# Hybrid decoder layer: RWKV head pairs with alpha and r side by side, r H of both heads in one product, the state's update in two halves of 64 columns

## The chip, the cores and the metric

The kernel runs on 1 core of one Trainium2 chip. The metric is the device time of one execution in microseconds (us). A core has five engines with a queue each: TensorE (PE; its weight loads are shown as PEld), VectorE (DVE), ScalarE (ACT), GpSimd (POOL) and SyncE (SP), which here issues all DMAs. Each works its instructions off in order, and waits on semaphores for the others. DVE, ACT and PE can reach PSUM, where matmuls put their results.

## The reference, cut to what matters

One layer: RMSNorm, one input projection whose columns go to a convolution group, a sparse attention group and an RWKV-7 group; an output projection; a gated MLP. 1024 tokens, all float32. The change lies in the RWKV group (4 heads of 64):

```python
def step(S, inp):
    r_t, w_t, k_t, v_t, kk_t, a_t = inp
    sa = jnp.einsum('bhvk,bhk->bhv', S, -kk_t)
    S = S * w_t[:, :, None, :] + sa[..., None] * (kk_t * a_t)[:, :, None, :] + v_t[..., None] * k_t[:, :, None, :]
    return S, jnp.einsum('bhvk,bhk->bhv', S, r_t)
```

The kernel does not scan 1024 tokens. It cuts them into 16 chunks of 64 and writes the recurrence within a chunk as matrices: with the decays multiplied in, alpha = -kk (shifted decay), r = r (decay), and "keys" k and kk*a divided by the decay, a chunk needs the masked products of keys with alpha (GA) and of keys with r (GR), the inverse of a triangular matrix taken from GA, and the state H at its start.

## The kernel before, in words

**Units.** The RWKV work is cut into four units (j, h): j is a pair of heads (128 channels), h a half of the tokens (8 chunks). Each unit has three steps, named in one string that orders the first phase: `lora r0 S00 conv taps V00 S01 keys q C00 V01 r1a cmp0 r1b cmp1 r1c S10 C01 V10 S11 C10 V11 C11`. S is `rwkv_prep` and `rwkv_mats`, V `rwkv_solve`, C `rwkv_chain`; the other names are projections (with L229's matmuls) and the convolution's 31 taps.

**S.** `rwkv_prep` loads k, r and v, makes the decays (L415 to L428), the norm of the keys (L437 to L446), alpha (L457, L458, into the right half of the tile VAc beside v), r times decay (L461) and the keys BK (L468, L469). `rwkv_mats` multiplies keys by alpha (L493, 16 products of 64 columns for 8 chunks and 2 heads), masks them into GA (L497), sends the lower corners to DRAM and back (L503, L506), and does the same for r into GR. It transposes VAc and BK into VA and KB (L517, L518). Then GpSimd inverts 32x32 triangles by 31 steps of two instructions, L528 and L530; DVE copies the result transposed (L532), and it goes to DRAM.

**V.** `rwkv_solve` loads the inverses back (L543 to L547) and does five groups of small matmuls (L550, L556, L563, L571, L575), with an ACT copy after each.

**C.** `rwkv_chain` goes through the 8 chunks: AT times H (L591), DVE adds into VA (L592), KB times VA (L596) is the state's update, which DVE adds to the decayed state (L601, L603); the output is GR times VA (L609) plus r times H (L611) for each head. H is 128x128 with a head in each diagonal block and zeros beside them. Group norm and gate follow (L617 to L638).

**What sets the order.** The kernel is written in a tile framework. While it is built, a scheduler gives each engine its queue by a timeline of its own: of the instructions that are ready there, the one with the highest priority goes next, and S, V and C carry a high priority. A tile is put into a free slot of its pool; RWKV tiles of 128x512 share 20 slots (`rb`). So an edit in `rwkv_prep` moves work of all groups in all queues. After the first phase come eight attention tiles, then the output projection, then the MLP (Strassen-like products of 7 instead of 8) up to the end.

**The convolution's taps.** Of its two channel halves DVE does one (L270, L272: 31 instructions of 128x1024); of the other, ACT scales each tap (L278) and POOL adds it (L274, L279: 60 adds of 128x512). A projection needs its weights split into a high and a low part: ACT writes `whi` (L120), DVE `wlo` (L121), both with 2 buffers.

Of the kernel before, what the change touches and what calls it, by code (L numbers as in the profile page):

```python
# [16 lines left out]
P = 128  # L17


class K:  # L20
# [370 lines left out]
    def rwkv_prep(self, j, h):  # L391
# [61 lines left out]

        for q in range(2):
            sl = slice(q * 256, q * 256 + 256)
            al = VAc[q][:, :, 1, :]
            v.scalar_tensor_tensor(al[:, :, 1:64], c3(kk[:, sl])[:, :, 1:64], -1.0, c3(Pt[:, sl])[:, :, 0:63], op0=ALU.mult, op1=ALU.mult)  # L457
            v.tensor_scalar(al[:, :, 0], c3(kk[:, sl])[:, :, 0], -1.0, None, op0=ALU.mult)  # L458
        u.r = self.rb([P, 8, 64], name="rP")
        u.AT = self._t(self.mc, [P, 8, 64], F32, "at", "AT")  # L460
        et(u.r, c3(rr), c3(Pt), op=ALU.mult)  # L461

# [18 lines left out]
    def rwkv_mats(self, u):  # L481
# [5 lines left out]
        u.GA, u.GR = [], []  # L487
        for x, G in enumerate((u.GA, u.GR)):
            pts = [self.bank(u.tp) for _ in range(2)]
            for c in range(8):  # L490
                for hp in range(2):
                    r = slice(hp * 64, hp * 64 + 64)
                    pe.matmul(pts[hp][:, c * 64:c * 64 + 64], u.BK[c // 4][r, c % 4].rearrange("p a t -> p (a t)"),  # L493
                              u.r[r, c, :] if x else u.VAc[c // 4][r, c % 4, 1, :], start=True, stop=True)
            for hp in range(2):
                Gm = self.rb([P, 8, 64], name="GR" if x else "GA")
                v.tensor_tensor(Gm, pts[hp].rearrange("p (a b) -> p a b", b=64),  # L497
                                self.gmask[:, x * 64:x * 64 + 64].unsqueeze(1).to_broadcast([P, 8, 64]), op=ALU.mult)
                G.append(Gm)
                if not x:  # L500
                    for blk in range(2):
                        p0 = blk * 16 + hp * 8
                        nc.sync.dma_start(dn[p0:p0 + 8].rearrange("p s t -> s p t"), Gm[64 + blk * 32:96 + blk * 32, :, blk * 32:blk * 32 + 32])  # L503
# [75 lines left out]
    def rwkv_chain(self, u):  # L579
# [7 lines left out]
        for c in range(8):  # L587
# [6 lines left out]
            if not last:  # L594
                pt = self.bank("rw")
                pe.matmul(pt[:, 0:P], KB, VA, start=True, stop=True)  # L596
# [8 lines left out]
            yo = (c // 2) * P  # L605
            for hp in range(2):
                x = slice(hp * 64, hp * 64 + 64)
                o = py[ro, yo + hp * 64:yo + hp * 64 + 64]
                pe.matmul(o, u.GR[hp][:, c, :], VA[:, x], start=True, stop=H is None)  # L609
                if H is not None:  # L610
                    pe.matmul(o, u.r[:, c, :], H[:, x], start=False, stop=True)  # L611
# [790 lines left out]
```

## Time and profile before

| | us |
|---|---|
| runs (3) | 1509.61, 1513.1, 1527.16; median 1513.1 |
| profiled execution, its own time | 1503.66 |
| its span | 1501.9 |
| PE / DVE / ACT / POOL busy | 1418.3 / 1006.5 / 682.5 / 498.9 |

The page of the profile has the busy time of each engine and a strip of 40 slices, each 37.5 us, with tenths of busy time. The first phase reaches to about 377 us, the attention tiles to 743, the output projection to about 860, and the MLP to the end. In a row of the timeline the two numbers are the start and the length in us of a run of equal instructions (x16 is 16 of them); the bracket is the idle time of the engine before it, with what ended it. A float32 matmul of the program shows as two matmul records. Line numbers are those of the kernel before.

### The profile page before, as it was taken

The page shows a single profiled execution, that of the slowest core. Times are in us where ns is not written, and L with a number is a line of the kernel's source. Part 1 is how long each engine was busy: PE and PEld are TensorE (multiplying, and loading weights), DVE is VectorE, ACT ScalarE, POOL GpSimd, SP SyncE. Part 2 cuts the span into 40 slices and gives each one's busy share as a digit, 9 for nine tenths or more (in the row PEclk, how much of TensorE's full clock was granted, in tenths as well). Part 3 has the DMA queues.
Part 4 walks back from the last instruction along what each step waited for, and adds up shares of the span by engine and source line. Part 5 has one row for each costly group of instructions (what it writes and reads, how often), then busy time and mean ns, then how long its engine had stood idle before and what let it go on. Part 6 is the DMA issues. An engine that isn't in the chain of part 4 may idle for free.

```text
span 1501.9 us, 22963 instructions
## 1 busy us (share of the span) xinstructions
PE 1418.3 (94%) x8025; PEld 1125.8 (75%) x8025; DVE 1006.5 (67%) x2171; ACT 682.5 (45%) x1361; POOL 498.9 (33%) x607
## 2 busy tenths in 40 slices
PE   6999688999899999999799899999999999999997
PEld 5887466777677777667588677788888888888886
DVE  6347696454577777689436876775775876666675
ACT  5431255534266555668523443333333344445463
POOL 1003787910432273240100133444443452113310
PEclk9999887999699999999999999999999999999999
DMA  6132223434812442553642122332332333986623
GB/s 186 36 113 74 46 77 96 148 88 120 227 26 72 143 136 74 163 171 104 182 155 78 52 80 80 106 113 91 106 112 84 106 113 125 390 284 212 203 92 112
DMA packets 206680, 186.71 MB, mean 124 GB/s; under 512 B 56355, under 2 KB 145764, under 8 KB 206564
## 3 DMA queue, kind: packets, MB, share of 16 engines
q1 hardware_dynamic: 206564, 185.24, 39.6%
q8 instruction: 63, 1.03, 0.3%
q14 instruction: 53, 0.43, 0.1%
HBM read 126.99 MB, written 58.20 MB: 123 GB/s over the span
## 4 chain that ended last, share of the span: by engine, by line
PE 80%; DVE 10%; DMA 3%; POOL 2%; issue 2%; ACT 1%; SPq 1%; DVEq 0%; POOLq 0%; ACTq 0%
PE mm L229 13%; PE gb L229 12%; PE rw L229 11%; PE ga L229 9%; PE gc L229 8%; PE tr L229 5%; PE tr L918 4%; PE av L926 4%; PE mm L893 2%; PE mm L894 2%; POOL sT L530 1%; DVE pp L897 1%; POOL sx L528 1%; DMA x<-in_x_dram 1%; DVE cacc L272 1%
## 5 line engine op out<-in xcount | busy, mean ns | idle before, releaser
L229 PE MATMUL mm<-hT,whi 128*128 128x512 f32 x608 | 200.5, 410 | 0.0
L229 PE MATMUL mm<-hT,wlo 128*128 128x512 f32 x304 | 125.3, 414 | 20.2 <-DVE wlo L121 20.2
L229 PEld LDWEIGHTS mm<-hT,whi 128*128 128x128 f32 x608 | 117.4, 195 | 28.3 <-issue 1.4
L921 ACT ACTIVATE pT<-tr 128x512 f32<-128x512 f32 (+1 forms) x152 | 79.2, 534 | 54.4 <-PE tr L918 52.7
L926 PE MATMUL av<-pT,V 128*64 128x128 f32 x1056 | 95.3, 289 | 2.3 <-ACT pT L921 2.3
L279 POOL TENSOR_TENSOR cacc<-cacc,ctap 128x512 f32<-128x512 f32 x60 | 91.8, 1552 | 14.8 <-ACT ctap L278 14.6
L1072 POOL TENSOR_TENSOR S<-wraw,wr 128x512 f32<-128x512 f32 x22 | 28.5, 1296 | 194.7 <-DVE or L107 93.5
L918 PE MATMUL tr<-idn,pp 128*128 128x128 f32 x528 | 91.2, 291 | 1.9 <-DVE pp L911 1.7
L121 DVE TENSOR_TENSOR sp<-rb,sp 128x512 fp32r<-128x512 f32 x66 | 57.3, 868 | 48.6 <-ACT sp L120 48.3
L229 PEld LDWEIGHTS mm<-hT,wlo 128*128 128x128 f32 x304 | 59.4, 196 | 38.2 <-DVE wlo L121 21.3
L229 PE MATMUL rw<-sp,sp 128*128 128x512 f32 x330 | 86.2, 389 | 0.0
L229 PE MATMUL tr<-sp,sp 128*128 128x512 f32 x330 | 85.9, 389 | 0.0
L229 PE MATMUL rw<-woh,mix 128*128 128x512 f32 x240 | 79.1, 406 | 5.3 <-DVE xn L994 5.3
L893 PE MATMUL mm<-KH,QS 128*128 128x512 f32 (+2 forms) x192 | 76.8, 406 | 5.8 <-DVE mx L897 3.6
L918 PEld LDWEIGHTS tr<-idn,pp 128*128 128x128 f32 x528 | 57.0, 143 | 31.6 <-issue 28.0
L926 PEld LDWEIGHTS av<-pT,V 128*64 128x64 f32 x1056 | 59.1, 138 | 28.8 <-issue 13.7
L120 ACT ACTIVATE sp<-rb 128x512 fp32r<-128x512 f32 x66 | 41.6, 630 | 74.4 <-PE tr L229 36.5
L121 DVE TENSOR_TENSOR sp<-b,sp 128x512 fp32r<-128x512 f32 x88 | 69.7, 802 | 6.0 <-ACT sp L120 5.9
L229 PEld LDWEIGHTS rw<-sp,sp 128*128 128x128 f32 x330 | 61.9, 188 | 13.2 <-ACT sp L120 0.4
L229 PEld LDWEIGHTS tr<-sp,sp 128*128 128x128 f32 x330 | 61.9, 188 | 12.9
L911 DVE TENSOR_SCALAR pp<-pp,sm 128x640 f32<-128x640 f32 (+7 forms) x128 | 68.3, 573 | 1.0
L904 ACT ACTIVATE pp<-pp,nm 128x640 f32<-128x640 f32 (+3 forms) x64 | 57.6, 902 | 23.8 <-DVE nm L902 22.5
(457 smaller groups left out, 3699.5 us busy)
## 6 DMA issues: line engine op xcount, KB each, us to landing
wr<-in_ffn_w_gate_dram SPq DMA_DIRECT2D x44, 256.0 KB
wraw<-in_ffn_w_up_dram SPq DMA_DIRECT2D x44, 256.0 KB
pdS<-prod SPq DMA_DIRECT2D x44, 256.0 KB
b<-pdS SPq DMA_DIRECT2D x44, 256.0 KB
rb<-tdT SPq DMA_DIRECT2D x44, 256.0 KB
pdA<-prod SPq DMA_DIRECT2D x33, 256.0 KB
b<-pdA SPq DMA_DIRECT2D x33, 256.0 KB
wraw<-in_w_in_dram SPq DMA_DIRECT2D x30, 256.0 KB
```

The source lines that it names most:

```text
L120: self.nc.scalar.activation(hi, src, AF.Copy)
L121: getattr(self.nc, eng).tensor_tensor(lo, src, hi.bitcast(F32), op=ALU.subtract)
L229: mm = lambda l, r, **k: self.nc.tensor.matmul(out, l, r, skip_group_check=more, **k)
L279: nc.gpsimd.tensor_tensor(t[:, o:o + 512], t[:, o:o + 512], z, op=ALU.add)
L893: pe.matmul(pts[g][:, 0:n], QS[:, r, g, :], KH[g][hf][:, ks], start=True, stop=False)
L894: pe.matmul(pts[g][:, 0:n], QS[:, r, g, :], KL[g][hf][:, ks], start=False, stop=True)
L904: s.activation(Ps[g], Ps[g], AF.Exp, bias=nm[:, g:g + 1], scale=-1.0, accum_out=sm[:, g:g + 1])
L911: v.tensor_scalar(Ps[g], Ps[g], sm[:, g:g + 1], None, op0=ALU.mult)
L918: pe.transpose(pt[:, o:o + P], Ps[g][:, kt * P:kt * P + P], self.idn)
L921: s.activation(pT[:, 0:n], pt[:, 0:n], AF.Copy)
L926: pe.matmul(av[g * 64:g * 64 + 64, r * P:r * P + P], self.V[kk // 2][:, kk % 2, vo + g * 64:vo + g * 64 + 64], pT[:, o:o + P], start=first ...
L1072: gp.tensor_tensor(t, x, y, op=op)
```

## The change

1. alpha is written by DVE into a new tile AR ([128, 4 chunks, 2, 64], two per unit); ACT copies it into VAc, and copies r into AR's other half. 2. `rwkv_mats` multiplies keys by alpha and r at once: per half unit q (4 chunks) and head one product of 128 columns, 16 per unit in place of 32 of 64 columns. The masks are 8 DVE instructions of 256 columns per unit in place of 4 of 512. 3. The state's update KB x VA is two products, with 64 columns of KB each. 4. r x H is one product of 128 columns for both heads, ahead of GR x VA, in place of two of 64.

```diff
--- before.py
+++ after.py
@@ -451,14 +451,18 @@
         et(k2, k2, rk, op=ALU.mult)
         e.tensor_scalar(tha, tha, 0.5, 0.5, op0=ALU.mult, op1=ALU.add)
 
+        u.AR = [self.rb([P, 4, 2, 64], name="AR") for _ in range(2)]
         for q in range(2):
             sl = slice(q * 256, q * 256 + 256)
-            al = VAc[q][:, :, 1, :]
+            al = u.AR[q][:, :, 0, :]
             v.scalar_tensor_tensor(al[:, :, 1:64], c3(kk[:, sl])[:, :, 1:64], -1.0, c3(Pt[:, sl])[:, :, 0:63], op0=ALU.mult, op1=ALU.mult)
             v.tensor_scalar(al[:, :, 0], c3(kk[:, sl])[:, :, 0], -1.0, None, op0=ALU.mult)
+            s.activation(VAc[q][:, :, 1, :], al, AF.Copy)
         u.r = self.rb([P, 8, 64], name="rP")
         u.AT = self._t(self.mc, [P, 8, 64], F32, "at", "AT")
         et(u.r, c3(rr), c3(Pt), op=ALU.mult)
+        for q in range(2):
+            s.activation(u.AR[q][:, :, 1, :], u.r[:, q * 4:q * 4 + 4, :], AF.Copy)
 
         et(kk, kk, tha, op=ALU.mult)
         u.BK = []
@@ -484,23 +488,23 @@
         dn = self.dram.tile([32, 32, 32], F32, name=f"dn{u.j}{u.h}")
         u.dt = self.dram.tile([16, 32, 4, 8], F32, name=f"dt{u.j}{u.h}")
         u.dtt = self.dram.tile([32, 8, 4, 32], F32, name=f"dtt{u.j}{u.h}")
-        u.GA, u.GR = [], []
-        for x, G in enumerate((u.GA, u.GR)):
+
+        u.GA, u.GR = ([self.rb([P, 8, 64], name=n) for _ in range(2)] for n in ("GA", "GR"))
+        for q in range(2):
             pts = [self.bank(u.tp) for _ in range(2)]
-            for c in range(8):
+            for c in range(4):
                 for hp in range(2):
                     r = slice(hp * 64, hp * 64 + 64)
-                    pe.matmul(pts[hp][:, c * 64:c * 64 + 64], u.BK[c // 4][r, c % 4].rearrange("p a t -> p (a t)"),
-                              u.r[r, c, :] if x else u.VAc[c // 4][r, c % 4, 1, :], start=True, stop=True)
-            for hp in range(2):
-                Gm = self.rb([P, 8, 64], name="GR" if x else "GA")
-                v.tensor_tensor(Gm, pts[hp].rearrange("p (a b) -> p a b", b=64),
-                                self.gmask[:, x * 64:x * 64 + 64].unsqueeze(1).to_broadcast([P, 8, 64]), op=ALU.mult)
-                G.append(Gm)
-                if not x:
-                    for blk in range(2):
-                        p0 = blk * 16 + hp * 8
-                        nc.sync.dma_start(dn[p0:p0 + 8].rearrange("p s t -> s p t"), Gm[64 + blk * 32:96 + blk * 32, :, blk * 32:blk * 32 + 32])
+                    pe.matmul(pts[hp][:, c * P:c * P + P], u.BK[q][r, c].rearrange("p a t -> p (a t)"),
+                              u.AR[q][r, c].rearrange("p a t -> p (a t)"), start=True, stop=True)
+            for x, G in enumerate((u.GA, u.GR)):
+                for hp in range(2):
+                    v.tensor_tensor(G[hp][:, q * 4:q * 4 + 4, :], pts[hp].rearrange("p (a b) -> p a b", b=P)[:, :, x * 64:x * 64 + 64],
+                                    self.gmask[:, x * 64:x * 64 + 64].unsqueeze(1).to_broadcast([P, 4, 64]), op=ALU.mult)
+        for hp in range(2):
+            for blk in range(2):
+                p0 = blk * 16 + hp * 8
+                nc.sync.dma_start(dn[p0:p0 + 8].rearrange("p s t -> s p t"), u.GA[hp][64 + blk * 32:96 + blk * 32, :, blk * 32:blk * 32 + 32])
         N = self.sN.rearrange("p (a b) -> p a b", b=32)
         for g in range(4):
             nc.sync.dma_start(N[g * 32:g * 32 + 32], dn)
@@ -593,7 +597,8 @@
             last = u.h == 1 and c == 7
             if not last:
                 pt = self.bank("rw")
-                pe.matmul(pt[:, 0:P], KB, VA, start=True, stop=True)
+                for x in (slice(0, 64), slice(64, 128)):
+                    pe.matmul(pt[x, 0:P], KB[:, x], VA, start=True, stop=True)
                 Hn = self.rH[c % 2]
                 for hp in range(2):
                     x = slice(hp * 64, hp * 64 + 64)
@@ -603,12 +608,11 @@
                         v.scalar_tensor_tensor(Hn[x, x], H[x, x], u.PC[x, c:c + 1], pt[x, x], op0=ALU.mult, op1=ALU.add)
             ro = slice((c % 2) * 64, (c % 2) * 64 + 64)
             yo = (c // 2) * P
+            if H is not None:
+                pe.matmul(py[ro, yo:yo + P], u.r[:, c, :], H, start=True, stop=False)
             for hp in range(2):
                 x = slice(hp * 64, hp * 64 + 64)
-                o = py[ro, yo + hp * 64:yo + hp * 64 + 64]
-                pe.matmul(o, u.GR[hp][:, c, :], VA[:, x], start=True, stop=H is None)
-                if H is not None:
-                    pe.matmul(o, u.r[:, c, :], H[:, x], start=False, stop=True)
+                pe.matmul(py[ro, yo + hp * 64:yo + hp * 64 + 64], u.GR[hp][:, c, :], VA[:, x], start=H is None, stop=H is None or hp == 1)
             H = None if last else Hn
         self.H = H
```

The scheduler's queues move with it. Three places follow, in the rows that the built programs have; a number after a name is that of a buffer, and lines after L460 stand 4 lower after the change in most places (L532 became L536, L528 L532, L530 L534).

POOL, the end of the first unit's inverse (S00); before:

```order
L528 TENSOR_TENSOR sx<-sN,sT 128x49
L530 TENSOR_TENSOR sT<-sT,sx 128x7x7
L528 TENSOR_TENSOR sx<-sN,sT 128x42
L530 TENSOR_TENSOR sT<-sT,sx 128x6x7
L528 TENSOR_TENSOR sx<-sN,sT 128x35
```

and after the change:

```order
L532 TENSOR_TENSOR sx<-sN,sT 128x49
L274 TENSOR_SCALAR cacc_1582<-cy_1515,par 128x1024
L534 TENSOR_TENSOR sT<-sT,sx 128x7x7
L279 TENSOR_TENSOR cacc_1582<-cacc_1582,ctap_1615 128x512
L279 TENSOR_TENSOR cacc_1582<-cacc_1582,ctap_1618 128x512
L532 TENSOR_TENSOR sx<-sN,sT 128x42
L279 TENSOR_TENSOR cacc_1582<-cacc_1582,ctap_1621 128x512
L534 TENSOR_TENSOR sT<-sT,sx 128x6x7
L279 TENSOR_TENSOR cacc_1582<-cacc_1582,ctap_1624 128x512
L532 TENSOR_TENSOR sx<-sN,sT 128x35
```

Before, all 62 instructions of the inverse stand in a row, and the first tap (L274) follows them. Now L274 and 13 taps of L279 stand among the last 13 of the 62.

DVE, the transposed copy of that inverse (tile sTT) and the splits of weights (wlo) about it; before:

```order
L257 SCALAR_TENSOR_TENSOR cy_1521<-ev_1455,mm_279_1535 128x512
L272 SCALAR_TENSOR_TENSOR cacc_1587<-cy_1389,par,cacc_1587 128x1024
L532 COPY sTT<-sT 128x256
L121 TENSOR_TENSOR wlo_2255<-wraw_2252,whi_2254 128x512
L272 SCALAR_TENSOR_TENSOR cacc_1587<-cy_1389,par,cacc_1587 128x1024
```

and after the change:

```order
L121 TENSOR_TENSOR wlo_2393<-wraw_2389,whi_2392 128x512
L272 SCALAR_TENSOR_TENSOR cacc_1581<-cy_1383,par,cacc_1581 128x1024
L443 COPY cum_2026<-rrn_2043 128x512
L536 COPY sTT<-sT 128x256
L121 TENSOR_TENSOR wlo_2400<-wraw_2396,whi_2399 128x512
```

The copy stood behind 14 of DVE's 30 taps of L272, and stands behind 28 now; five wlo splits, the norm of unit S01 (L439 to L443) and three evictions of keys (L686) were moved ahead of it. On PE, 14 projection matmuls stood between unit S01's L437 and the first product of V00 (L550), and 127 do now.

PE, the decays and the key norm of unit S10 (products L415, L419, L437, L446); before, two pieces of the queue:

```order
L575 MATMUL rw_2942<-W_2931,sN 64x64 x8
L415 MATMUL rw_3413<-lora_771,lw_w 128x512
L229 MATMUL mm_591_3245<-hT_120,wlo_3242 128x512
...
L437 MATMUL rw_3432<-bones,cum_3422 128x2 x4
L768 MATMUL tr_566_3138<-hx_3036,w2k 64x64
L229 MATMUL mm_606_3341<-hT_120,whi_3337 128x512
```

and after the change:

```order
L579 MATMUL rw_2931<-W_2920,sN 64x64 x8
L415 MATMUL rw_3402<-lora_771,lw_w 128x512
L419 MATMUL rw_3406<-lora_771,lw_w 128x512
L437 MATMUL rw_3421<-bones,cum_3411 128x2 x4
L446 MATMUL rw_3444<-idn,cum_3411 128x128 x4
L843 MATMUL mm_4522<-kcmp_4433,q_816_4515 128x128 x4
L897 MATMUL mm_4542<-KH_4487,QS_4517 128x256
```

Between these four products of S10 stood 72 projection matmuls, and nothing stands there now; the projections are all ahead of L415, and the first attention products follow L446.

## Rows read from the trace of the kernel before

**Rows 1.** Stretches: length, then busy us of each engine, granted clock, DMA share.

```profile
157.00:172.00 15.00, 2.49 (x15) 1.84 (x14) 1.04 (x2) 0.63 (x1) 11.47 (x40) 0.65 0.00 0
172.00:208.00 36.00, 27.79 (x195) 21.56 (x196) 36.00 (x34) 15.10 (x23) 28.32 (x17) 0.81 0.38 84
240.00:377.00 137.00, 137.00 (x792) 107.17 (x792) 62.45 (x160) 62.51 (x118) 57.75 (x93) 0.96 0.42 120
377.00:396.00 19.00, 15.18 (x74) 13.01 (x73) 9.65 (x21) 1.59 (x4) 7.79 (x11) 0.58 0.90 252
```

**Rows 2.** Timeline of PE: products of keys and transposes, in S00 and in S10.

```profile
120.08 2.00 PE L493 MATMUL pm<-VAc,BK 64*128 64x64 f32 x16
138.48 0.60 PE L517 MATMUL pm<-idn,BK 128*128 128x128 f32 x4
383.75 5.66 PE L493 MATMUL rw<-VAc,BK 64*128 64x64 f32 x29
396.88 1.06 PE L517 MATMUL rw<-idn,VAc 128*128 128x128 f32 x4
```

**Rows 3.** Timeline of PE: part of a chain step; three of V00's products.

```profile
408.75 0.38 PE L596 MATMUL rw<-VA,KB 128*128 128x128 f32 x2
409.06 0.33 PE L609 MATMUL rw<-VA,GR 128*64 128x64 f32 x2
177.19 1.19 PE L550 MATMUL rw<-DF,GA 32*32 32x32 f32 x32 [0.54 <-DMA DF<-dt]
188.13 0.97 PE L563 MATMUL rw<-sN,VA 64*64 64x64 f32 x26
189.12 0.92 PE L571 MATMUL rw<-VA,GA 64*64 64x64 f32 x13
```

**Rows 4.** Timeline of POOL: inverse S00 (first and 23rd of 62), then taps.

```profile
134.59 0.40 POOL L528 TENSOR_TENSOR sx<-sN,sT 128x31 f32<-128x31 f32 x1 [38.06 <-DMA sN<-dn]
156.51 0.29 POOL L528 TENSOR_TENSOR sx<-sN,sT 128x60 f32<-128x60 f32 x1
177.45 26.36 POOL L279 TENSOR_TENSOR cacc<-cacc,ctap 128x512 f32<-128x512 f32 x15
255.09 1.28 POOL L279 TENSOR_TENSOR cacc<-cacc,ctap 128x512 f32<-128x512 f32 x1
```

**Rows 5.** Timeline of DVE: mask, taps, the copy, a later tap; norms of S01 and S10.

```profile
127.02 0.69 DVE L497 TENSOR_TENSOR GA<-pm,gmask 128x512 f32<-128x512 f32 x1 [2.40 <-PE pm L493]
136.00 6.56 DVE L272 SCALAR_TENSOR_TENSOR cacc<-cy,par,cacc 128x1024 f32<-128x1024 f32 x5
170.96 0.70 DVE L532 COPY sTT<-sT 128x256 f32<-128x256 f32 x1 [14.70 <-POOL sT L530]
198.56 2.37 DVE L272 SCALAR_TENSOR_TENSOR cacc<-cy,par,cacc 128x1024 f32<-128x1024 f32 x1
208.77 0.42 DVE L443 COPY cum<-rrn 128x512 f32<-128x512 f32 x1
369.22 0.43 DVE L443 COPY cum<-rrn 128x512 f32<-128x512 f32 x1
```

**Rows 6.** Timeline of PE: a wait behind wlo, S10's products, entry to the output projection.

```profile
172.31 0.80 PE L229 MATMUL mm<-hT,wlo 128*128 128x512 f32 x1 [12.82 <-DVE wlo L121]
352.38 1.12 PE L415 MATMUL rw<-lora,lw_w 32*128 32x512 f32 x2
381.78 2.05 PE L474 MATMUL rw<-cum,bones 128*128 128x512 f32 x2 [3.64 <-DVE cum L472]
714.77 1.12 PE L636 MATMUL rw<-lora,lw_w 64*128 64x512 f32 x2
729.75 0.80 PE L229 MATMUL rw<-woh,mix 128*128 128x512 f32 x1
749.55 0.80 PE L229 MATMUL rw<-woh,mix 128*128 128x512 f32 x1 [5.29 <-DVE xn L994]
```

**Rows 7.** Groups by line, ACT: busy us, mean ns, idle before.

```profile
L742 ACT ACTIVATE KC<-mm 64x256 f32<-64x256 f32 x16 | 6.1, 380 | 4.2 <-PE mm L229 4.0
```

## The prediction, made before the changed kernel was run

> **What bounds the kernel now.** The table of busy times comes first: PE is busy 1418.3 of 1501.9 us, so time is lost where PE waits and won where a stretch bound by PE gets shorter. Then the stretches [rows 1]: in one of 137 us (240 to 377) PE never rests, and each us of matmuls removed there is a us. From 157 to 172 PE works 2.5 us of 15; from 172 to 208 it has 27.8 of 36, while DVE is busy all 36. In the timeline of POOL and DVE [rows 4, 5] the reader is to see why. The first unit's inverse is 62 small instructions on POOL. Beside DVE's taps the first 22 take 21.9 us (134.59 to 156.51), 1.0 us each. Then DVE's queue arrives at the copy of the inverse's result (L532) and waits 14.7 us, and without it POOL does the other 40 in 14.5 us, 0.36 us each. A weight split (wlo) stands right behind the copy, so PE waits 12.8 us [rows 6]. Afterwards POOL's own taps run against DVE's: 1.76 us each in place of 1.28 [rows 4], and DVE's taps take 2.37 in place of 1.31 [rows 5].
>
> **A. One product of keys for alpha and r.** The first L493 of S00 is 16 records in 2.00 us; less the last one's 0.27, the tail that a record shows, that is 0.115 us from start to start, for 64 columns. The transposes with 128 columns take 0.11 [rows 2]. So a record of 64 columns is paced by something that 128 columns don't lengthen, and 32 records replace 64 at one price: 7.4 us become 3.7 per unit. In S10 L493 runs at a granted clock of 0.58, mostly the lower level of 1.2 GHz, after PE had waited 3.6 us [rows 1, 6]: 0.187 us each, 12.0 us for 64; 128 columns there show 0.213 [rows 2], so 32 take 6.8. S00's gain lies ahead of DVE's wait and is lost in it; S01 gives 3.7, S10 5.2, S11 (priced as S00) 3.7. **Minus 12.6.** The other bound is that twice the columns cost twice the time: 0.
>
> **B. State and r H.** KB's product of two records is followed by GR's after 0.31 us [rows 3]. Two halves make four records of 128 columns. L563, which alternates between the two heads' columns of the array, goes at 0.030 us a record, and L571, which stays in one place, at 0.058 [rows 3]. If the halves run side by side as in L563, two records' time stays; if not, four take 4 x 0.115 = 0.46, so 0.15 x 30 chain products = +4.5. The halves alternate as L563 does: I take 0. The r H product has half the records with twice the columns: 0, or down to -3 if the 0.11 floor above is what paces it.
> The Trainium skill (TensorEngine Tiling (Array Packing), Key Properties) says that a change of tiling mode drains the array. By that rule the 128x128 update among 128x64 products pays two drains a step, and halves would save them; the 0.31 us against 0.23 for two records at the pace of A leaves some 0.08 for one, and the sum would be 5 us lower by the rule.
>
> **C. Copies and masks.** 16 ACT copies of 128x256 cost about 0.4 us each, by the nearest row, 0.38 for 64x256 [rows 7]; ACT is busy 62.5 us of 137 in the PE-bound stretch [rows 1], so they are hidden. If that cover were gone, 4 x 0.4 = 1.6 us a unit would stand ahead of the G products, 6 us in all. Eight masks of 256 columns replace four of 512 on DVE: below 1 us a unit, beside PE. GA now needs r as well, and its last mask stands in DVE's queue behind the first three taps, near 134 us in place of 127.02 [rows 5]. From the mask to POOL's start were 7.6 us, so the inverse starts at about 141.5 instead of 134.59 [rows 4].
>
> **D. The queues about the first inverse.** This is the largest move. DVE now comes to the copy behind 28 taps instead of 14. From 136.00 to the start of its wait (156.26) DVE did 12 taps with their company, 1.69 us per tap; 26 more from 136 and the norm of S01 (2 us) bring it to the copy at about 182 to 184. POOL, beside a busy DVE, has then done 42 of the 62 at 1.0 us. The rest is 20 x 0.36 = 7 us, and the taps placed among the last ones, L274 and 13 of L279, at 1.28 to 1.35 since DVE stands still: 18 to 19 us. The copy starts at about **210**; DVE waits some 27 us and PE some 25, twice the old wait. But at 210 DVE has finished the norm of S01 (L443) and all taps but two, and before it ended that same L443 at 209 [rows 5], since half of its taps had run against POOL's. **Plus 1.** Bounds: if DVE pauses on PE before the copy and POOL does 20 of the 42 at 0.36, the copy starts 13 us earlier; if all 62 and the taps go at the slow pace (62 x 1.0 + 14 x 1.76 = 87), it starts at 228, +18.
> The Trainium skill (SBUF — State Buffer, SBUF: two separate sides) calls the port that VectorE and GpSimd share a lock held for a whole instruction, the loser blocked. By that rule each POOL step beside taps waits for a tap, 1.28 to 1.31 us against the 1.0 measured on average, and the copy would start some 3 us later, the sum by as much.
>
> **E. V00 and S10.** V00's products were done inside the DVE-bound stretch, for nothing. Their place is now behind the copy and 17 us of projections further, in the PE-bound stretch: L550 and L556 1.19 each, L563 1.0, L571 and L575 32 x 0.058 each [rows 3] = 7.1, and about one us of C00's first steps. **Plus 8.** In S10 the four products L415 to L446 stand in a row, so PE sits through the dependent work of ACT and DVE between them: 17.3 us from L415 to the end of the copy L443 [rows 5, 6], less 3 us of PE's own work, is the upper bound, 14; the lower is the 3.6 that PE waits in that unit now [rows 6]. Part of the 17.3 was L437 waiting for its turn behind projections, so I take 7: **plus 3.4.** The lower clock that follows a wait there (377 to 396) [rows 1] would be met in either kernel.
>
> **F. Entry to the output projection.** From the gate product L636 to the first output product are 15.0 us [rows 6]: group norm, store to DRAM, reload, split. PE filled them with attention work. Now about 5 us of it is left there, since the chain's end moved back in the queue, and the output products come in one block behind it: 7 us more idle, against the 5.3 us wait for x [rows 6], whose loads now go out ahead of the need. **Plus 1**, -3 to +7.
>
> **Sum.** -12.6 + 0 + 0 + 1 + 8 + 3.4 + 1 = -0.2 against the profiled execution's 1503.7, so 1503.5. The median shown (1513.1) lies 9.4 above the profiled one, the lowest run 6. I forecast **1510 us**, no change. This kernel's measurement tells about 2%, 30 us, from no change.
>
> **The rivals.**
> 1. The inverse's end becomes the bound (slower). Place: DVE's wait at the copy of S00. Each us that the copy starts after 210 is a us of idle PE, and the mechanism decides from about 215. For it: POOL's taps at 1.76 beside DVE [rows 4], and a PE that idled comes back at the lower clock (0.65 in the stretch with the wait) [rows 1]. At the slow bound it gives 1510 + 18 = 1528, and with 10 us of work at half the clock behind the wait 1533. Only with S10's upper bound (+7) and more such work does it come to 2%, 1543. Against: DVE stands still in that wait, and alone POOL went three times as fast. Chance 0.22, a quarter of it above 2%.
> 2. Taps and inverse come apart (faster). DVE's excess in 172 to 208 vanishes (1.06 us a tap), and the inverse ends early, at 197: -13 in D, -5 in B if the halves save time: about 1490. For it: DVE is 100% busy there. Against: the wait moves to the copy. Chance 0.13, a fifth of it past 2%.
> 3. The merged product saves nothing, since 128 columns double a record (the change doesn't do what it says): +12.6, 1522. Against: the transposes' pace [rows 2]. Chance 0.07.
> The forecast, within 1% of 1510, has 0.58.
>
> **The numbers.** Range 1490 to 1533: from the second rival to most of the first, leaving out 2 in 10. Within 2%: 0.58 + 0.07 + 0.22 x 3/4 + 0.13 x 4/5 = 0.92; slower 0.05; faster 0.03.
>
> **What would show it.** A: L498 in 32 records a unit at 0.11 us. D: the copy L536 waiting 20 to 35 us on POOL, PE idle behind it at about 186 to 211, few taps of 2.4 us on DVE after it. E: V00 behind 240 us; a gap of 5 to 10 us in PE between L415 and L446 of S10. F: no wait for x near 750. Wrong would be a copy start before 195 or after 220, or projections that end more than 10 us from 377.

## The result, and the profile after

The change ran in **1485.35 us** (median of 6 runs, 1479.4 to 1496.25) against 1511.36 us for the kernel before on the same chip (6 runs): ratio **0.9849, 95% interval 0.9819 to 0.9879**. That is 1.5% faster and below the range of the forecast (1490 to 1533). The profiled execution has a span of 1477.5 us in place of 1501.9, 24.4 us less; PE's granted clock is 0.971 in place of 0.964. Both profiled executions lie at the fast end of their kernel's (before: 1503.66 us); the change's six go from 1479.4 us at a granted clock of 0.971 to 1496.25 us at 0.960.

Where the 24.4 us are is read from PE's timeline alone. An instruction's share of PE's queue is the time from its start to the start of the next, less the wait noted on the next. Added up, these shares are PE's **work**, the noted waits its **idle time**; both sums and some 9 us behind the last matmul make the span. The idle time has in it the 4.4 us (with the change 5.1) ahead of the first matmul. This account is what the expectations below call the ledger.

| PE, us | before | after | difference |
|---|---|---|---|
| products of keys (L493, L498) | 36.5 | 17.0 | -19.5 |
| chain: AT H, state, r H, GR | 8.0 + 9.7 + 8.6 + 9.0 | 3.3 + 8.2 + 7.9 + 8.6 | -7.3 |
| all other work | 1347.3 | 1344.7 | -2.6 |
| idle, up to the last projection | 40.8 | 41.5 | +0.7 |
| idle, from there to the first output product | 15.9 | 16.6 | +0.7 |
| idle, from there to the end | 17.2 | 20.7 | +3.5 |

By place: the projections end at 360.9 (before 377.8), the first output product starts at 706.95 (before 729.75 [rows 6]), and from there to the end both kernels take about as long (770.6 us, before 772.2).

These 29.4 us of work are not all matmuls that were removed, since work is counted in time. A mean granted clock of 0.964 over 1501.9 us is 108 us at the lower level of 1.2 GHz, one of 0.971 over 1477.5 us is 86; by the clock in the two traces, 82.2 and 52.7 us of PE's work lie at that level. The largest part of the difference is in the stage from the last projection to the first output product (first row: before):

```profile
377.80:729.75 351.95, 335.63 (x2851) 249.45 (x2851) 267.89 (x918) 210.72 (x487) 116.73 (x198) 0.94 0.43 126
360.90:706.95 346.05, 325.71 (x2874) 236.43 (x2874) 276.65 (x950) 219.38 (x506) 116.58 (x198) 0.97 0.43 127
```

These rows have the length of a stretch, then the busy us of PE, PEld, DVE, ACT, POOL, then PE's granted clock, DMA share, GB/s. What the lower level costs is seen in one kind of record on both sides of a rise of the clock, in the changed kernel: 0.43 us from start to start at 184 us, 0.23 at 189.

```profile
184.14 1.05 PE L229 MATMUL mm<-hT,whi 128*128 128x512 f32 x2
184.99 0.63 PE L229 MATMUL mm<-hT,wlo 128*128 128x512 f32 x1
...
188.80 0.62 PE L229 MATMUL mm<-hT,whi 128*128 128x512 f32 x2
189.26 0.39 PE L229 MATMUL mm<-hT,wlo 128*128 128x512 f32 x1
```

At this price 29.5 us less work at the lower level are some 14 of the 29.4 us, and the removed records the other 16: an estimate, as other records can have another price.

The stretches that answer to [rows 1], in the same view: the one without work, the one at DVE's pace, the one at PE's, and the passage to attention.

```profile
166.00:181.00 15.00, 0.19 (x2) 0.14 (x1) 0.94 (x2) 3.63 (x6) 13.51 (x30) 0.67 0.01 3
181.00:229.00 48.00, 36.99 (x175) 26.70 (x176) 46.65 (x47) 22.58 (x39) 41.77 (x32) 0.75 0.37 101
229.00:361.00 132.00, 131.41 (x816) 102.25 (x816) 60.60 (x142) 66.06 (x124) 68.25 (x101) 0.99 0.43 124
361.00:379.00 18.00, 10.47 (x74) 7.85 (x72) 8.59 (x27) 7.40 (x16) 4.48 (x11) 0.63 0.86 247
```

The wait in the first of them has another cause than before. PE, DVE, ACT and POOL of the changed kernel, from the timeline (start, length, engine, line, and in brackets the wait ahead with what ended it):

```profile
180.89 1.19 PE L229 MATMUL mm<-hT,whi 128*128 128x512 f32 x2 [14.81 <-DVE ev L690]
212.82 1.19 PE L554 MATMUL rw<-DF,GA 32*32 32x32 f32 x32
224.11 2.04 PE L478 MATMUL pm<-cum,bones 128*128 128x512 f32 x2 [4.95 <-DVE cum L476]
...
180.06 0.69 DVE L690 TENSOR_TENSOR ev<-mm,ev 128x512 fp32r<-128x512 f32 x1 [16.14 <-ACT ev L689]
201.30 1.50 DVE L443 COPY cum<-rrn 128x512 f32<-128x512 f32 x1
202.89 0.69 DVE L536 COPY sTT<-sT 128x256 f32<-128x256 f32 x1
...
176.16 0.72 ACT L278 ACTIVATE ctap<-cy,par 128x512 f32<-128x512 f32 x1 [19.16 <-POOL cacc L279]
179.44 0.58 ACT L689 ACTIVATE ev<-mm 128x512 fp32r<-128x512 f32 x1
...
139.16 0.72 POOL L532 TENSOR_TENSOR sx<-sN,sT 128x31 f32<-128x31 f32 x1 [42.47 <-DMA sN<-dn]
163.96 0.31 POOL L532 TENSOR_TENSOR sx<-sN,sT 128x76 f32<-128x76 f32 x1
173.47 1.20 POOL L274 TENSOR_SCALAR cacc<-cy,par 128x1024 f32<-128x1024 f32 x1
174.86 2.48 POOL L279 TENSOR_TENSOR cacc<-cacc,ctap 128x512 f32<-128x512 f32 x2
192.38 1.22 POOL L534 TENSOR_TENSOR sT<-sT,sx 128x24 f32<-128x24 f32 x1
202.47 0.39 POOL L534 TENSOR_TENSOR sT<-sT,sx 128x8 f32<-128x8 f32 x1
```

ACT has scaled two tiles for POOL's taps (ctap, two buffers) and waits 19.16 us for the first to come free, since POOL's taps stand behind 49 of the 62 steps of the inverse. Behind that ctap and two more stands L689; DVE's L690 waits for it, and PE for L690. So DVE stops at 164, before its copy (L536), which then starts at 202.89 with no wait noted, as POOL's last step ends. POOL, alone, does the next 25 steps from 163.96 to 173.47, 0.38 us each; from there on the steps of the inverse take turns with taps.

In S10 the row of dependent products shows two waits, at the entry to the output projection there are two more, for the split of the chain's last result (mix), in place of the wait for x of [rows 6]:

```profile
369.92 1.86 PE L437 MATMUL rw<-bones,cum 128*128 128x2 f32 x8 [3.02 <-ACT cum L434]
374.79 1.12 PE L446 MATMUL rw<-idn,cum 128*128 128x128 f32 x4 [3.01 <-DVE cum L443]
...
706.95 0.71 PE L229 MATMUL rw<-woh,mix 128*128 128x512 f32 x1 [3.19 <-ACT mix L120]
725.87 0.79 PE L229 MATMUL rw<-woh,mix 128*128 128x512 f32 x1 [5.81 <-ACT mix L120]
```

The products themselves: L498 of S00 and S10, 16 records each, 1.71 and 1.68 us ([rows 2]: 2.00 for 16 of S00, and S10's at the lower level). Of the chain, the first fence has rows of the kernel before, the second of the change.

```profile
129.53 1.71 PE L498 MATMUL pm<-AR,BK 64*128 64x128 f32 x16
389.50 1.68 PE L498 MATMUL rw<-AR,BK 64*128 64x128 f32 x16
```

```profile
253.39 0.39 PE L596 MATMUL rw<-VA,KB 128*128 128x128 f32 x2
253.71 0.33 PE L609 MATMUL rw<-VA,GR 128*64 128x64 f32 x2
...
269.88 0.43 PE L591 MATMUL rw<-rH,AT 128*64 128x128 f32 x2
270.24 0.74 PE L229 MATMUL mm<-hT,whi 128*128 128x512 f32 x2
```

```profile
274.13 0.32 PE L595 MATMUL rw<-rH,AT 128*64 128x128 f32 x1
274.14 0.32 PE L612 MATMUL rw<-rH,rP 128*64 128x128 f32 x1
274.29 0.27 PE L595 MATMUL rw<-rH,AT 128*64 128x128 f32 x1
274.30 0.27 PE L612 MATMUL rw<-rH,rP 128*64 128x128 f32 x1
274.50 0.74 PE L229 MATMUL mm<-hT,whi 128*128 128x512 f32 x2
...
282.19 0.43 PE L595 MATMUL rw<-rH,AT 128*64 128x128 f32 x2
282.46 0.38 PE L612 MATMUL rw<-rH,rP 128*64 128x128 f32 x2
282.77 0.72 PE L229 MATMUL mm<-hT,whi 128*128 128x512 f32 x2
...
326.66 0.44 PE L601 MATMUL rw<-VA,KB 128*64 128x128 f32 x4
326.94 0.39 PE L615 MATMUL rw<-VA,GR 128*64 128x64 f32 x4
```

AT H alone held PE from 269.88 to 270.24, 0.36 us. With r H beside it, both hold it from 274.13 to 274.50, 0.37 us: their records alternate. That is an even chunk. In an odd one the two go one after the other, from 282.19 to 282.77, 0.58 us. The kernel has AT H written to partitions 64 to 127 of PSUM in every chunk, r H to 0 to 63 in even chunks and to 64 to 127 in odd ones. In the trace the records alternate in all 12 even chunks in which the two follow each other, and in none of the 16 odd ones. The update in halves is followed by GR after 0.28 us, in one piece after 0.32.

### The profile page after: what moved, and what is told of

It is laid out like the page before. It is cut to its first block, busy times and chain, and to the rows that moved or that the text cites. A ratio compares the mean times of both kernels' runs of the same rounds, so it can differ in the third digit from the quotient of the medians.

```text
span 1477.5 us, 22767 instructions
## 1 busy us (share of the span) xinstructions
PE 1388.7 (94%) x7897; PEld 1095.2 (74%) x7897; DVE 1002.7 (68%) x2187; ACT 686.9 (46%) x1377; POOL 499.2 (34%) x607
## 4 chain that ended last, share of the span: by engine, by line
PE 79%; DVE 8%; POOL 4%; DMA 3%; ACT 2%; issue 2%; SPq 1%; ACTq 0%; DVEq 0%; POOLq 0%
PE gb L229 13%; PE mm L229 12%; PE rw L229 10%; PE ga L229 9%; PE gc L229 8%; PE tr L229 5%; PE tr L922 5%; PE av L930 4%; PE mm L897 2%; PE mm L898 2%; POOL sT L534 1%; POOL sx L532 1%; DVE pp L901 1%; POOL cacc L279 1%; DVE pp L915 1%
## 5 line engine op out<-in xcount | busy, mean ns | idle before, releaser
L229 PE MATMUL mm<-hT,whi 128*128 128x512 f32 x608 | 200.3, 409 | 19.6 <-DVE ev L690 14.8
L279 POOL TENSOR_TENSOR cacc<-cacc,ctap 128x512 f32<-128x512 f32 x60 | 85.1, 1429 | 12.7 <-ACT ctap L278 12.4
L922 PEld LDWEIGHTS tr<-idn,pp 128*128 128x128 f32 x528 | 55.9, 141 | 30.5 <-issue 29.1
L915 DVE TENSOR_SCALAR pp<-pp,sm 128x640 f32<-128x640 f32 (+7 forms) x128 | 76.5, 638 | 0.9
L120 ACT ACTIVATE sp<-rb 128x512 fp32r<-128x512 f32 x66 | 41.6, 630 | 74.1 <-PE tr L229 36.5
L532 POOL TENSOR_TENSOR sx<-sN,sT 128x60 f32<-128x60 f32 (+24 forms) x124 | 48.0, 387 | 63.0 <-DMA sN<-dn 54.9
```

What stands on the lines that cost most here:

```text
L120: self.nc.scalar.activation(hi, src, AF.Copy)
L229: mm = lambda l, r, **k: self.nc.tensor.matmul(out, l, r, skip_group_check=more, **k)
L279: nc.gpsimd.tensor_tensor(t[:, o:o + 512], t[:, o:o + 512], z, op=ALU.add)
L532: v_.tensor_tensor(x, N[:, q, q + 1:32].unsqueeze(2).to_broadcast([P, n, w]), Tm[:, q, 0:w].unsqueeze(1).to_broadcast([P, n, w]), op=ALU.mult)
L915: v.tensor_scalar(Ps[g], Ps[g], sm[:, g:g + 1], None, op0=ALU.mult)
L922: pe.transpose(pt[:, o:o + P], Ps[g][:, kt * P:kt * P + P], self.idn)
```

## Experiments

All were timed beside the kernel before. The table has the ratio to it with its 95% interval, and from each profile the span, PE's work, the part of it at the lower clock, PE's idle time, the part of the idle time among the output products, and how many of the 1288 matmuls of attention stand in PE's queue, by the program's order, behind the chain's last product (the gate of the last unit's output).

| run | median us | ratio | span | work | of it at 1.2 GHz | idle | of it at output | rows behind |
|---|---|---|---|---|---|---|---|---|
| before | 1508 to 1511 | 1 | 1501.9 | 1419.0 | 82.2 | 73.9 | 5.3 | 75 |
| the change | 1485.4 | 0.9849 [0.9819, 0.9879] | 1477.5 | 1389.6 | 52.7 | 78.8 | 9.0 | 41 |
| 1 merge only | 1504.4 | 0.9982 [0.9961, 1.0003] | 1502.5 | 1397.2 | 61.0 | 96.2 | 17.0 | 0 |
| 2 chain only | 1508.3 | 0.9997 [0.9973, 1.0021] | 1508.1 | 1420.2 | 92.4 | 78.9 | 7.3 | 90 |
| 3 merge, not S00 | 1483.9 | 0.9839 [0.9806, 0.9872] | 1479.0 | 1393.7 | 47.4 | 76.3 | 6.0 | 67 |
| 4 merge, S00 only | 1526.4 | 1.0120 [1.0092, 1.0148] | 1524.2 | 1420.4 | 86.5 | 94.2 | 4.7 | 67 |
| 5 two products | 1498.8 | 0.9933 [0.9899, 0.9968] | 1494.0 | 1400.4 | 56.3 | 84.6 | 6.4 | 41 |
| 6 no r H merge | 1502.3 | 0.9938 [0.9918, 0.9958] | 1500.1 | 1395.4 | 62.5 | 95.8 | 18.2 | 0 |
| 7 masks by head | 1488.7 | 0.9843 [0.9814, 0.9872] | 1484.3 | 1391.2 | 53.6 | 83.3 | 15.1 | 16 |
| 8 change, not S00 | 1478.2 | 0.9771 [0.9743, 0.9799] | 1475.7 | 1390.8 | 45.1 | 75.9 | 4.6 | 89 |
| 9 no halves | 1500.6 | 0.9960 [0.9926, 0.9994] | 1492.6 | 1394.3 | 65.5 | 89.3 | 8.2 | 24 |
| 10 halves swapped | 1481.0 | 0.9813 [0.9772, 0.9853] | 1478.0 | 1391.0 | 56.2 | 78.0 | 2.6 | 67 |
| 11 first taps on POOL | 1482.4 | 0.9826 [0.9798, 0.9853] | 1481.1 | 1388.6 | 51.7 | 82.6 | 9.2 | 41 |
| 12 run 8, taps on POOL | 1473.5 | 0.9768 [0.9736, 0.9801] | 1470.3 | 1388.0 | 37.2 | 73.3 | 5.2 | 89 |

**1 and 2: the parts apart.** Run 1 has the change's prep and mats and the chain of before; run 2 the reverse:

```diff
-                for x in (slice(0, 64), slice(64, 128)):
-                    pe.matmul(pt[x, 0:P], KB[:, x], VA, start=True, stop=True)
+                pe.matmul(pt[:, 0:P], KB, VA, start=True, stop=True)
...
-                pe.matmul(py[ro, yo:yo + P], u.r[:, c, :], H, start=True, stop=False)
...
+                    pe.matmul(o, u.r[:, c, :], H[:, x], start=False, stop=True)
```

> Only the first part: alpha and r side by side and the merged products of 128 columns, the state's update and r H as in the kernel before. Ledger theory (from the two traces: merged products give back 19.5 us of PE's queue, the chain products 6.8 us, and PE's idle time grows by only 4.6 us): 15 us less, about 1496. The forecast on record (merge -12.6, V00's new place, S10's serial start and the inverse together +13.4): no change, about 1511. If the chain's halves were what counts: no change, 1511.

> Only the second and third part: state update in two halves of 64 columns, r H of both heads in one product; the products of keys as in the kernel before. Their queues around the first inverse stand as before. Ledger theory: 7 us less, about 1504. The forecast on record: no change, 1511. The rule of the Trainium skill (TensorEngine Tiling (Array Packing), Key Properties: a change of tiling mode drains the array): 5 us less, about 1506.

By the ratios neither gains alone: 3 us (interval -0.5 to 6) and nothing; together 23. So the parts don't add, and my theory that they do fell here (1496 and 1504 expected). Run 1 did lose 22 us of work; its idle time grew by as much, 23.1 us within attention (before 12.0, the change 8.0) and 17.0 at the output products. Up to the last projection it is the change's twin (361.5 against 360.9). Run 2's chain cost 30.5 us of work in place of 35.2, but its products of keys 3.9 more, and its idle time grew by 5.0. Work doesn't add either: -21.8 and +1.2 us against -29.4. By the estimate above 9.9 of run 1's 21.8 us are the lower clock, and run 2 lost 4.7 by it; without that the parts give 11.9 and 3.5 us, and the change 15.7.

**3 and 4: S00 and the other units apart.** S00's mask products set the start of the first inverse, and with it the places of taps and V00. The diff is that of run 3; run 4 has == in it. GA and GR are split by the same condition.

```diff
+        if (u.j, u.h) != (0, 0):
+            u.AR = [self.rb([P, 4, 2, 64], name="AR") for _ in range(2)]
...
+        else:
...
+                al = VAc[q][:, :, 1, :]
```

> The merged products in S01, S10 and S11 alone; S00 and the chain as in the kernel before, so that the taps, the first inverse and V00 keep their old places on VectorE, GpSimd and TensorE. Ledger theory: three units' savings (3.9 + 7.9 + 3.9) with no added idle time: 15 us less, about 1496, as much as with S00. The forecast on record: -12.6, about 1498.5, 12 us faster than with S00, whose moves it priced at +13. If the new places were the gain: at most 4 us less, 1507.

> The merged product in S00 alone; S01, S10, S11 and the chain as in the kernel before. The copy of the first inverse now stands behind 26 taps, V00 behind 17 us more of projections, as in the whole change. Ledger theory: S00's 3.9 us against 4.6 us of added idle time: no change, 1511. The forecast on record: the moves cost 13 us, about 1523. If the new places were the gain: 10 to 15 us less, about 1499.

With the old places the merge of three units gives 24 us, all that the whole change gives; with the new places S00's alone costs 18 (0.9 to 1.5%). For run 4 the forecast on record was nearest (1523), for run 3 none was low enough. Run 3's products of keys take 14.7 us less, its whole work 25.3, of which 34.8 us less at the lower clock are some 16. Run 4's idle time is 20 us above the kernel before: 7.9 us more among the projections, 6.7 in attention, 7.1 ahead of products of keys. Two waits of 16.41 and 8.94 us and one in S11 are the largest:

```profile
182.88 1.22 PE L229 MATMUL mm<-hT,whi 128*128 128x512 f32 x2 [16.41 <-DVE ev L719]
227.68 0.79 PE L229 MATMUL mm<-hT,wlo 128*128 128x512 f32 x1 [8.94 <-DVE wlo L121]
...
562.39 3.67 PE L526 MATMUL rw<-rP,BK 64*128 64x64 f32 x16 [6.02 <-DVE GA L530]
```

**5: the price of the product.** AR, copies and masks stay, but each product is two again:

```diff
-                    pe.matmul(pts[hp][:, c * P:c * P + P], u.BK[q][r, c].rearrange("p a t -> p (a t)"),
-                              u.AR[q][r, c].rearrange("p a t -> p (a t)"), start=True, stop=True)
+                    for x in range(2):
+                        pe.matmul(pts[hp][:, c * P + x * 64:c * P + x * 64 + 64], u.BK[q][r, c].rearrange("p a t -> p (a t)"),
+                                  u.AR[q][r, c, x], start=True, stop=True)
```

> The whole change, but each merged product is done as two products of 64 columns out of the same tile AR; copies, masks and chain are those of the change. Theory of the records (a product of 128 columns goes at the pace of one of 64, so the merge gives back its 32 records a unit): TensorE's queue 19.5 us longer than with the change, about 1505. If what gained was the order of the queues around it and not the products: as the change, 1485. Attention rows left behind the chain's end: 41, as in the change, so the entry to the output projection should wait as long as there (9 us).

Products of keys 33.2 us in place of 17.0: +16.2 us, PE's whole work +10.8, and 13.5 us of time. S10's, at the lower clock, have 9.7 of the 16.2 (13.43 us, with the change 3.75); S00's 64 records took 6.5 us where 32 of the change took 3.81. 16 records of 64 columns take what 16 of 128 take, and more (2.00 against 1.71 above). The waits at the output products were 6.4 us, not 9. The order wasn't the change's about the first inverse: here V00 waits for its inverse (second row). So what the run shows by itself is the price of the records, and the 13.5 us have other waits in them.

```profile
120.69 2.00 PE L499 MATMUL pm<-AR,BK 64*128 64x64 f32 x16
...
186.20 1.91 PE L555 MATMUL rw<-DF,GA 32*32 32x32 f32 x32 [16.33 <-DMA DF<-dt]
```

**6, 7, 9 and 10: the chain's parts and the order.** 6 is the change with r H in two products (the r H lines of the diff above), 9 with the update in one. 7 and 10 compute the same with the same instructions, written in another order; the first piece is run 7's, the second run 10's:

```diff
-            for x, G in enumerate((u.GA, u.GR)):
-                for hp in range(2):
+            for hp in range(2):
+                for x, G in enumerate((u.GA, u.GR)):
...
-                for x in (slice(0, 64), slice(64, 128)):
+                for x in (slice(64, 128), slice(0, 64)):
```

> The change without its third part (r H again as two products of 64 columns a step). If the parts simply add: 1486 to 1488, since r H cost 7.9 us of TensorE's queue with the change and 8.3 before. Theory of idle time (what TensorE waits depends on where the order leaves the end of the chain: no row of attention is left behind it here, as with part 1 alone, where TensorE waited 17 us at the entry to the output projection and 23 us within attention): 15 to 20 us more than the change, about 1502.

> The change with the eight masks of a unit written head by head (GA, GR of one head, then of the other) and nothing else: the same instructions in another order, which moves the end of the chain to 16 rows of attention from the end in place of 41. If the gain is the work that was taken out: as the change, 1485, TensorE's work 1390 us. Theory of idle time: the same work, and 5 to 15 us more idle time in attention and at the entry to the output projection, 1490 to 1500.

> The change without its second part (the state's update again as one product of 128 columns). If parts add: 1 to 2 us more than the change, 1487. Theory of idle time: 24 rows of attention are left behind the chain's end, between the runs with 16 (15.1 us of waits among the output products) and 41 (9.0 and 6.4 us), so 11 to 14 us of waits there and 1490 to 1496 in all.

> The change with the two halves of the state's update written in the other order and nothing else: the same instructions, and 67 rows of attention behind the chain's end in place of 41. Theory of idle time: 4 to 6 us of waits among the output products in place of 9, TensorE's work as with the change (1390), so 1481 to 1485. If the position of the chain's end does not set these waits: 9 us again.

The theory of idle time held in 6 (1502.3 for 1502) and 10 (1481.0, the low end of its range; waits at the output products of 2.6 us, none of them for mix, for 4 to 6). In 7 it held for the waits at the output products (15.1 us) and not for the time: 1488.7 is below its range, and the ratio (0.9843) is the change's (0.9849). It was too low for 9 (1500.6 for 1490 to 1496), where the waits at the output products were 8.2 us, not 11 to 14, and attention's rose to 19.7 (with the change 8.0) instead. With the change itself, work is within 6 us in all five kernels; idle time goes from 78 to 96 us. In runs 1, 6, 7 and 10 PE comes to the output products and finds (from the timeline, one fence for each):

```profile
736.10 0.79 PE L229 MATMUL rw<-woh,mix 128*128 128x512 f32 x1 [13.93 <-ACT mix L120]
```
```profile
732.17 0.80 PE L229 MATMUL rw<-woh,mix 128*128 128x512 f32 x1 [14.34 <-ACT mix L120]
```
```profile
716.47 0.80 PE L229 MATMUL rw<-woh,mix 128*128 128x512 f32 x1 [11.80 <-ACT mix L120]
```
```profile
727.83 0.47 PE L229 MATMUL rw<-woh,mix 128*128 128x512 f32 x1 [2.24 <-DVE xn L998]
```

The mixture that is split there comes from the chain's end. With 0 and 16 attention rows left, PE runs dry for 11.8 to 14.3 us; with 67 rows, in run 10, it never waits for mix, only for x (xn). Two swaps that change no work put the waits at the output products at 15.1 and 2.6 us. That they moved the time is not shown: both intervals overlap the change's, and run 7's profiled span is 7 us longer where the change's own executions differ by 17 us.

**8: the change without S00's part.** The edit is that of run 3, on the change.

> The whole change but for S00, whose products and masks stay as in the kernel before. The places of taps, inverse and V00 are then the old ones, and 89 rows of attention are left behind the chain's end. Ledger theory: TensorE's work as in the run without S00's merge (1393) less what the chain parts give (2 to 7), idle time as there (77): about 1479, 6 us faster than the change. If S00's own merged products are worth what they took out of TensorE's queue (4 to 5 us) and its new order nothing: 1490.

1478.2, where the ledger said 1479. The interval lies wholly below the whole change's. S00's merged products save 4.2 us of products of keys, but with them PE's whole work is only 1.2 us less, with 7.6 us more of it at the lower clock, and its idle time 3 us more: in their new places they gain nothing.

**11 and 12: the stop behind ScalarE's taps.** The diff is run 11's; run 12, on run 8, has 2 for 4.

```diff
-                        nc.scalar.activation(z, y[:, o + d:o + d + 512], AF.Copy, scale=w)
+                        if d <= 4:
+                            nc.gpsimd.tensor_scalar(z, y[:, o + d:o + d + 512], w, None, op0=ALU.mult)
+                        else:
+                            nc.scalar.activation(z, y[:, o + d:o + d + 512], AF.Copy, scale=w)
```

> The change, with the scaling of GpSimd's first four taps (8 of 60 tiles) done by GpSimd itself in place of ScalarE, so that no tap that waits for GpSimd stands in ScalarE's queue ahead of the copies of keys and weights. Attention and chain keep the order that they have with the change (41 rows behind the chain's end). With the change TensorE waited 14.8 us at 166 to 181 behind ScalarE's third tap. Theory of the pause: that stop is also what lets GpSimd, alone, do the inverse at 0.36 us a step; without it VectorE goes on, the inverse ends later than 202 (at 215 to 235), and TensorE waits as long in all up to the end of the projections (38 to 48 us against 41.5): 1478 to 1492. Rival: the stop is a pure loss, its 14.8 us are saved: about 1470.

> The change without S00's part (the run that was fastest so far), with the scaling of GpSimd's first two taps done by GpSimd. There VectorE's stop is at the copy of the inverse, and what ScalarE's taps add is a wait of 4.5 us behind ctap at 193. If that wait is a loss: 3 to 5 us less than that run, about 1474. If it only moves: 1478, and if GpSimd's four more steps delay its taps, up to 1482.

The stop in run 11 came back 28 us later (DVE from 192 to 211), at the next ctap, and PE idled 45.2 us up to the last projection in place of 41.5. The inverse ended at 225 in place of 203, and the time is in the range of the theory of the pause (1478 to 1492), not the rival's 1470:

```profile
212.56 1.22 PE L229 MATMUL mm<-hT,whi 128*128 128x512 f32 x2 [21.49 <-ACT whi L120]
...
225.19 0.70 DVE L539 COPY sTT<-sT 128x256 f32<-128x256 f32 x1
...
208.43 0.72 ACT L281 ACTIVATE ctap<-cy,par 128x512 f32<-128x512 f32 x1 [28.80 <-POOL cacc L282]
```

So the 14.8 us are not a loss that can be struck out: while DVE goes on, POOL is slow. In run 12, where DVE stops at the copy in any case, the edit gives 5 us in the span and in the median, as the forecast had it if the wait is a loss (1474); by the ratios, 0.9768 and 0.9771, no gain is shown. Both are 2.3% below the kernel before, the fastest here.

## Why the prediction was wrong

The sum was -0.2 us; from profile to profile it measured -24.4. Four of its steps failed: the place of S00's gain in A, the size of B, the copy's place in D with V00's price in E, and the clock, which had no term.

**A, the merged products, was right in price and wrong in place.** 32 records take 3.75 to 3.81 us of PE's queue where 64 took 7.17, 0.118 us each in place of 0.112, as was taken from [rows 2]; in run 5 64 of them took 6.5 us in S00. S01 gave 3.3 (8.99 to 5.64; forecast 3.7), S11 5.0 (8.79 to 3.81; forecast 3.7), S10 7.8 (11.54 to 3.75; forecast 5.2). S10's is partly a loan: the stretch at the lower level is still there (a clock of 0.63 at 361 to 379, before 0.58 in the last of [rows 1]), but now the dependent products L415 to L446 (5.4 us in place of 3.3) and the first of attention lie in it. The step "S00's gain lies ahead of DVE's wait and is lost in it" failed in this account: S00 gave 3.4 us (7.17 to 3.81), and idle time up to the last projection grew by 0.7, all of it ahead of the first matmul. As time it is no gain: run 8, without it, is faster.

**B, the chain, was mis-sized: 0 forecast, -7.3 measured.** I counted records and not what stands beside them. r H needs only H, so in one product, ahead of GR, it is issued with AT H, and in even chunks the two alternate in the time of one: AT H went from 8.0 us to 3.3, with the two-product form (run 6) it was 7.1. That the halves of PSUM decide it is read from the trace; no run moved them. The halves as such gave the update 1.5 us (9.7 to 8.2; 9.4 without halves, run 9). The drain rule that the prediction cites from the Trainium skill (TensorEngine Tiling (Array Packing), Key Properties) points the right way, 0.28 us to the next product in place of 0.32, but its 5 us were 1.5; what gained most was not in it.

**D and E, the queues about the first inverse, failed at one step**: "26 more from 136 and the norm of S01 (2 us) bring it to the copy at about 182 to 184 ... The copy starts at about 210". I followed DVE's queue and POOL's, not ACT's. ACT's two ctap buffers stop it at the third tile, and through L689 and L690 stop DVE at 164, 19 us earlier than I had it. The stop is 16 us, not 27, and POOL does 25 of its fast steps there, 0.38 us each. It started at 139.16 (141.5 forecast) and its last step ended at 202.9, so the copy started at 202.9, not 210, with no wait on record. L443, which I had left at 209, came at 201.3. So PE's idle time up to the last projection grew by 0.7 us, where D (1), E's V00 (8) and the lost S00 (3.7) stood for 12.7. V00 did move, though to 212.8, not behind 240: into the stretch of 181 to 229, where PE is busy 37.0 of 48 us, and not into the one where it never rests. Why DVE was faster after its stop (7.5 us less up to L443) I read from the trace and did not test: POOL's steps and taps, in turn, got in its way less than POOL's taps back to back in [rows 4]. The Trainium skill's rule on the shared port (SBUF — State Buffer, SBUF: two separate sides) had each step wait for a tap; the steps between taps from 181.6 to 198 fit it (1.20 to 1.23 us), the first 24, beside DVE's taps, went at 1.03 on average. Run 11 shows the exchange itself: take the stop away, and the inverse ends 22 us later.

**The clock had no term.** Of the stretch at S10 the prediction says that its lower clock "would be met in either kernel". It was, but for 17 us in place of 27, and from the last projection to the first output product 16.5 us of PE's work lie at the lower level in place of 38.6, in the whole kernel 52.7 in place of 82.2. By the estimate above that is some 14 us of time, more than any term of the sum was off by. Why the stretches are fewer and shorter is open: the places of the waits changed everywhere at once.

**E's S10 and F were about right.** S10 waits 6.6 us in its row of products (3.6 before): +3.0, forecast +3.4, and 6.0 of it lie between L415 and L446, in the 5 to 10 us gap that was named. At the output products +3.7, forecast +1 within -3 to +7, and there was no wait for x.

**The second rival was the nearest**: 1490, by an earlier copy and faster halves. Its sizes were half right (copy at 202.9, not 197; chain -7.3, not -5), it had 0.13, and the products of S00 were missing in it. In the chain it was luck: it gave the 5 us to the halves, which made 1.5.

**What the terms had in common** is that the forecast took the order after 400 us as settled. Run 4 seems to bear out my price for the moves (+13): with S00's merge alone they cost 18. But 13.8 of its 20 us of idle time lie in attention and ahead of products of keys in S11, for which I had no term, so the near size is luck. With all parts together S00's part costs 3 to 7 us by the medians (run 8 against run 10 and the change; the intervals of 8 and 10 overlap). 22 to 25 us of saved work came out as 3 us of time (run 1), 6 (run 9), 9 (run 6) or 24 (run 3), by the ratios. At the output products the cause of the waits is shown: few rows left behind the chain's end, 15 to 18 us with 0 and 16 rows, 3 to 7 with 67 to 90. Between them the count doesn't decide: 8.2 us with 24, 6.4 to 9.2 with 41. Within attention (8 to 23 us idle) it is open; no single place accounts for it.

## What to carry to other kernels

Follow every in-order queue up to the stop that you price, the one of the engine that only feeds a helper too: its small ring of buffers can stop it before the wait that you are looking at. Split a forecast into PE's work at full clock, which here added up over the parts to within 1 us by estimate, the work that falls at the lower clock, and the idle time, which didn't add up. If a scheduler re-orders the whole program after each edit, give these two a range from edits like it before calling a 1% change good or bad: idle time was 78 to 96 us over the change and its four near variants, 78 to 83 over the two that change no work. A product that needs an early operand is worth moving ahead of those that wait, beside another of the same shape that is written to the other half of PSUM's partitions.

## What the hardware showed unexpectedly

- Products of 64 rows took PE's queue 0.112 us a record with 64 columns (S00 of the kernel before) and 0.118 with 128 (S00 of the change): half the columns saved little or nothing.
- Two products with the same moving H and the same 128x64 shape of weights (AT H, r H), issued together, held PE for 0.37 us where they are written to different halves of PSUM's partitions and for 0.58 where to the same half; one alone held it for 0.36.
- 82.2 us of PE's work before and 52.7 after the change lay at the granted clock's lower level, where a 512-column record took 0.43 us in place of 0.23.
